# Latent attention by keys: scores with keys on partitions, the maximum as a product row, no turned probabilities

## The chip, the cores and the metric

The kernel runs on one core of a Trainium2 chip. A core has a matrix engine (PE, with a separate weight load PEld), a vector engine (DVE), a scalar engine (ACT), a general engine (POOL) and DMA engines whose queues are issued from SP, ACT and POOL. The metric is the device time of one execution in microseconds; three executions of the kernel before gave 1923.1 to 1924.48 us with a median of 1923.17 us.

## The reference, cut to what matters

The model has two blocks. The change touches one part of the second block, the latent attention: 8 heads, 512 queries of the sequence, 768 keys (512 of the sequence and 256 of a context), head size 96 (64 from a latent, 32 rotary), value size 64. Cut from the reference:

```python
qa_n, qa_r = mla_q(cq, g_cq[i], w_uq[i])
ka_n, va = mla_kv(ckv, g_ckv[i], w_ukv[i])
ka = jnp.concatenate([ka_n, jnp.broadcast_to(ka_r, ka_n.shape[:-1] + (MLA_ROPE,))], axis=-1)
...
# block_attention, for every head, with mla_scale = 96 ** -0.5:
#   softmax over the 768 keys of (q k^T * mla_scale), then times v
```

The result of every head is multiplied with a gate (silu of a projection called za) and goes on into the output projection. Next to it stands a neighbourhood attention over the same sequence, with its own queries, keys and gates, which runs after the latent attention in the kernel.

## The kernel before, in words

Products that must be exact to about single precision are split: every operand is a high and a low part, and one product is three matrix multiplies (`mm3`, L130 to L132), high by high, high by low and low by high. Smaller products whose operands aren't split go through `mm` (L127) in plain single precision; each of these is two records in the trace. A transpose is a multiply with a unit matrix called `ident`, a part of a tile that the trace names `cst`.

`latent()` works on 4 pairs of heads. For each pair `keys(pr)` computes the keys of both heads (96 rows of which 32 are copied by POOL), as a high and a low tile `kT`. For each pair and each tile of 128 queries `queries(pr, t)` transposes the queries and splits them into `qT`. Then, for each of the 32 combinations of pair, query tile and head:

- `scores(n)` multiplies 128 queries (on partitions) with 768 keys, three multiplies of 512 and three of 256 columns, into a tile of two banks (`sc`). DVE reduces it to the negative maximum (L1699), and ACT takes the exponential with that maximum as bias and adds up the sums (L1701).
- `turn(n)` turns the probabilities P so that keys come onto partitions: six transposes (L1709), copied out of the banks by ACT (L1711, four tiles) and DVE (L1713, two tiles) as PT.
- `pv(n)`, once for both heads of a pair, multiplies PT with the values `va`, 12 products of 128 columns, the two heads on the two halves of the partitions. When a pair is done the reciprocals of its sums (DVE, L1728) are spread by small products to all rows (`spread`, L272, L273 and L127 with `rT`) and multiplied in.

Beside it there is work that has no part in the latent attention, the fills: projections of the block's input, written behind `latent()` in the code in the order `A G10 Q K G00 V` (gate za, one further gate, queries, keys, another gate, values of the neighbourhood attention). They use a bank of their own (`fl`). The order of instructions on each engine is not that of the code: a scheduler with a time model places them, so that a fill can stand between steps of the latent attention. Gate blocks are 24 multiplies of 512 columns that end in a tanh on ACT (L1650); the tile `zaT` receives gate za.

Tiles live in pools with a fixed number of buffers for each tag (`b8`: 3, `kt`: 5, `P`: 2 and so on). A tile that finds no free buffer makes its first writer wait for the last reader of an older one.

Of the kernel before, what the change touches and what calls it, by code (L numbers as in the profile page):

```python
# [34 lines left out]
PB2=6  # L35
PXE=1
# [5 lines left out]
MPS=dict(sc=2,po=1,fl=1)  # L42
MKT=5
MP=2
MPT=4
MQT=4
MQ1=5
# [31 lines left out]
def body(ctx, tc, a, stop=None, dump=None):  # L79
# [1432 lines left out]
    xd = dram.tile([128, 4, 1024], F32, name="xd")  # L1512
    nc.scalar.dma_start(xd, x)
# [13 lines left out]
    pm = pools3["u2"] = Pool("pm", "right", {"kr": 3, "kt": MKT, "P": MP, "PT": MPT, "b12": 1, "u2": 2, "qt": MQT, "q1": MQ1})  # L1527
# [103 lines left out]
    def tok_fill(x0, dst, scale=1.0):  # L1631
        for i in range(2):
            w = w3.pair(x0 + 2 * i)
            for t0, nt, p in tok_block(w, 256, hT, tag="fl"):
# [8 lines left out]
    def gate_fill(x0, z):  # L1643

        for m in range(4):
            p = ps(tag="fl")
# [20 lines left out]
    def latent():  # L1667
        kT, qT, PP, PT, sums = {}, {}, {}, {}, {}
        subs = [(pr, t, i) for pr in range(4) for t in range(4) for i in range(2)]

        def keys(pr):
            ks = [[pm("kt", [96, 768], F32R, "kT") for _ in range(2)] for _ in range(2)]
# [5 lines left out]
            for i in range(2):  # L1678
                kT[2 * pr + i] = ks[i]
                for j in range(2):  # L1680
                    G.tensor_copy(ks[i][j][64:96], krT[64 - 32 * j:96 - 32 * j])

        def queries(pr, t):
            p = ps((128, 4, 128), tag="tn")
            for i in range(2):
                T.transpose(p[:96, i], qtok[pr][:, t, i], ident)
            q = qT[pr, t] = [pm("qt", [96, 2, 128], F32R, "qT") for _ in range(2)]
            evac_hl(q[0], q[1], p[:96, :2])

        def scores(n):  # L1690
            pr, t, i = subs[n]
            k, q = kT[2 * pr + i], qT[pr, t]
            p = ps((128, 1024), tag="sc")[:, :768]
            if t + i == 0:
                sums[pr] = sm.tile([128, 8], F32, name=nm("sx"), tag="sx8")
            m = sm.tile([128, 1], F32, name=nm("mx"), tag="mx1")
# [418 lines left out]
```

## Time and profile before

| | before |
|---|---|
| median of three executions | 1923.17 us (1923.1 to 1924.48) |
| the profiled execution | 1923.06 us, of which the span of the trace is 1921.3 us |
| PE busy | 1743.1 us, 91% of the span |
| DVE, ACT, POOL busy | 672.0, 496.5 and 238.6 us |
| from the first query transpose to the end of the latent attention | 1453.60 to 1656.40 us |
| multiplies in this stretch (records) | 1541 |

The span runs from the first to the last instruction of the trace; what lies outside it is 1.76 us. A row of the trace's timeline gives a start and a duration; multiplies are pipelined, so the price of one is the distance between the starts of two, not its duration. In a row with a bracket, the number in it is the time that the engine had stood idle, and the name behind the arrow is what ended that.

### The profile page before, as it was taken

The page shows a single profiled execution, that of the slowest core. Times are in us where ns is not written, and L with a number is a line of the kernel's source. Part 1 is how long each engine was busy: PE and PEld are TensorE (multiplying, and loading weights), DVE is VectorE, ACT ScalarE, POOL GpSimd, SP SyncE. Part 2 cuts the span into 40 slices and gives each one's busy share as a digit, 9 for nine tenths or more (in the row PEclk, how much of TensorE's full clock was granted, in tenths as well). Part 3 has the DMA queues.
Part 4 walks back from the last instruction along what each step waited for, and adds up shares of the span by engine and source line. Part 5 has one row for each costly group of instructions (what it writes and reads, how often), then busy time and mean ns, then how long its engine had stood idle before and what let it go on. Part 6 is the DMA issues. An engine that isn't in the chain of part 4 may idle for free.

```text
span 1921.3 us, 24683 instructions
## 1 busy us (share of the span) xinstructions
PE 1743.1 (91%) x10244; PEld 1081.6 (56%) x10244; DVE 672.0 (35%) x1392; ACT 496.5 (26%) x973; POOL 238.6 (12%) x265
## 2 busy tenths in 40 slices
PE   6998999989999897988888889787899999999998
PEld 5984579963433232322323223222387888888878
DVE  5696686550110101111010110100444333544665
ACT  4335534521000000000000000000545444344433
POOL 2371101000000000000000000000003111333351
PEclk9998999989999999999999999999999999999999
DMA  6322613468999999999999999999622202332232
GB/s 214 105 88 94 192 56 100 175 264 369 425 426 427 426 425 428 424 427 427 425 425 427 427 425 426 427 426 425 242 72 55 56 23 58 89 96 85 79 112 86
DMA packets 95760, 498.39 MB, mean 259 GB/s; under 512 B 6565, under 2 KB 56577, under 8 KB 67233
## 3 DMA queue, kind: packets, MB, share of 16 engines
q1 hardware_dynamic: 90656, 479.06, 62.7%
q0 software_dynamic: 3408, 11.93, 1.9%
q10 hardware_dynamic: 1584, 5.83, 0.8%
q8 instruction: 80, 1.31, 0.3%
q14 instruction: 32, 0.25, 0.0%
HBM read 490.08 MB, written 5.67 MB: 258 GB/s over the span
## 4 chain that ended last, share of the span: by engine, by line
PE 50%; DMA 40%; DVE 5%; ACT 2%; issue 1%; POOL 1%; SPq 0%; DVEq 0%; ACTq 0%; POOLq 0%
DMA we<-in_expert_w_dram 37%; PE ps L127 21%; PE ps L130 8%; PE ps L131 8%; PE ps L132 8%; PE ps L1709 1%; DMA w<-in_ca_wkv_dram 1%; DMA w<-in_w_out_dram 1%; DVE wl L230 1%; PE ps L1867 1%; PE ps L748 1%; ACT wh L229 1%; DMA voff<-vb 1%; DVE qkc L526 1%; POOL sq L458 0%
## 5 line engine op out<-in xcount | busy, mean ns | idle before, releaser
L127 PE MATMUL ps<-we,xe 128*64 128x512 f32 x2048 | 460.7, 597 | 62.7 <-DMA we<-in_expert_w_dram 62.6
L127 PEld LDWEIGHTS ps<-we,xe 128*64 128x64 f32 x2048 | 142.6, 137 | 355.3 <-issue 263.6
L127 PE MATMUL ps<-we,hT 128*64 128x512 f32 x1024 | 233.4, 598 | 29.4 <-DMA we<-in_expert_w_dram 22.8
L127 PEld LDWEIGHTS ps<-we,hT 128*64 128x64 f32 x1024 | 69.8, 136 | 162.8 <-issue 129.7
L229 ACT ACTIVATE wh<-w 128x1024 fp32r<-128x1024 f32 (+4 forms) x100 | 103.9, 1041 | 119.4 <-PE ps L131 74.9
L1303 DVE TENSOR_TENSOR hid<-hid,ps 128x512 f32<-128x512 f32 x32 | 22.0, 687 | 322.1 <-PE ps L127 300.6
L1345 DVE SCALAR_TENSOR_TENSOR y<-ps,gate,y 64x512 fp32r<-64x512 f32 x32 | 24.0, 749 | 313.0 <-ACT y L1344 313.0
L1311 ACT ACTIVATE hT<-ps 128x512 f32<-128x512 f32 x32 | 19.1, 597 | 423.2 <-PE ps L1309 423.2
L301 POOL DMA_DIRECT2D gg<-in_rows_dram x2 | 1.1, 547 | 903.2 <-DMA we<-in_expert_w_dram 903.2
L230 POOL TENSOR_TENSOR wl<-w,wh 128x1024 fp32r<-128x1024 f32 (+1 forms) x34 | 82.7, 2433 | 232.1 <-ACT wh L229 209.5
L230 DVE TENSOR_TENSOR wl<-w,wh 128x1024 fp32r<-128x1024 f32 (+4 forms) x62 | 82.6, 1334 | 69.9 <-ACT wh L229 67.3
L1344 ACT ACTIVATE y<-ps,gate 64x512 fp32r<-64x512 f32 x32 | 21.8, 682 | 260.7 <-PE ps L127 247.6
L130 PE MATMUL ps<-hTh,wh 128*128 128x512 f32 x192 | 76.7, 399 | 1.7 <-ACT va L1624 1.7
L131 PE MATMUL ps<-hTl,wh 128*128 128x512 f32 x192 | 76.0, 396 | 0.0
L132 PE MATMUL ps<-hTh,wl 128*128 128x512 f32 x192 | 75.9, 396 | 0.0
L127 PEld LDWEIGHTS ps<-otT,xn 128*128 128x128 f32 x512 | 60.4, 194 | 24.3 <-issue 22.2
L130 PE MATMUL ps<-wh,hTh 128*128 128x256 f32 (+1 forms) x224 | 68.0, 303 | 0.1
L131 PE MATMUL ps<-wl,hTh 128*128 128x256 f32 (+1 forms) x224 | 67.1, 300 | 0.0
L127 PE MATMUL ps<-otT,xn 128*128 128x128 f32 x512 | 66.0, 284 | 1.0 <-ACT otT L1250 1.0
L132 PE MATMUL ps<-wh,hTl 128*128 128x256 f32 (+1 forms) x224 | 65.6, 298 | 0.0
L1262 DVE TENSOR_TENSOR xe<-ps,cols 128x512 f32<-128x512 f32 (+1 forms) x18 | 10.2, 598 | 144.3 <-PE ps L127 144.3
L1302 ACT ACTIVATE hid<-ps 128x512 f32<-128x512 f32 x32 | 19.1, 596 | 158.4 <-PE ps L127 158.4
(570 smaller groups left out, 3367.4 us busy)
## 6 DMA issues: line engine op xcount, KB each, us to landing
we<-in_expert_w_dram SPq DMA_DIRECT2D x171, 2048.0 KB, 34.4
we<-in_expert_w_dram SPq DMA_DIRECT2D x42, 1024.0 KB, 34.4
w<-in_w_in_dram SPq DMA_DIRECT2D x48, 512.0 KB, 3.8
w<-in_w_mod_dram SPq DMA_DIRECT2D x24, 512.0 KB, 4.3
w<-in_w_out_dram SPq DMA_DIRECT2D x16, 512.0 KB, 3.6
w<-in_ca_wkv_dram SPq DMA_DIRECT2D x8, 512.0 KB, 5.0
wcv<-in_ctx_kv_dram SPq DMA_DIRECT2D x2, 2048.0 KB, 21.4
bm<-in_bias_dram POOLq DMA_DIRECT2D x16, 256.0 KB, 3.2
```

The source lines that it names most:

```text
L127: T.matmul(out, l, r, start=st, stop=sp)
L130: T.matmul(out, L[0], R[0], start=st, stop=False)
L131: T.matmul(out, L[0], R[1], start=False, stop=False)
L132: T.matmul(out, L[1], R[0], start=False, stop=sp)
L229: S.activation(h, w, AF.Copy)
L230: (G if (self.ns % 3 == 2 if self is ws else W3E(self.ns)) else V).tensor_sub(l, w, h.bitcast(F32))
L526: V.scalar_tensor_tensor(o, u[:, 6 + j:518 + j], conv(m, j), o, op0=OP.mult, op1=OP.add)
L748: T.transpose(pp[:, j], st[u][hf][:, tsl(j)], ident)
L1303: V.tensor_mul(h, h, pu)
L1344: S.activation(Y[q][r, 2 * d], p[r], AF.Copy, scale=g)
L1345: V.scalar_tensor_tensor(Y[q][r, 2 * d + 1], p[r], g, Y[q][r, 2 * d].bitcast(F32), op0=OP.mult, op1=OP.subtract)
L1709: T.transpose(p[:, j], P[:, tsl(c0 + j)], ident)
```

## The change

- Scores are computed with keys on partitions: a unit is a pair of heads and one half (256) of the queries, and for each of 6 tiles of 128 keys there are six multiplies of 256 columns, three for each head, both heads side by side in one bank. The exponential goes from there straight to P, without bias and without a sum, and P is multiplied with the values as it stands. The turned probabilities (`turn`, PT) are gone.
- The maximum that was the bias comes first, in products of its own: `peak` multiplies the high parts alone, queries on partitions, 512 and 256 columns, into a bank pair (`mx`) that exists once; DVE reduces it (L1710), and `peak_rows` turns the negative maxima into two rows (two small products with `ident`, an ACT copy, L1716) that stand as rows 96 and 97 under the queries. The keys have in the same rows a 1 for their head and a 0 for the other, so that the product adds the maximum.
- The sums: DVE adds the P tiles of a unit (five additions, L1744); `close` adds over partitions with a product of ones (L127), takes the reciprocal of all 128 x 256 (L1752) and multiplies it in (L1756). `spread` isn't used here any more.
- Buffers: the queries of a whole pair lie in one tile, pairs 0 and 2 in the pool `p3` (`b4`), pairs 1 and 3 in `p3m` (`b8`, 3 buffers), where `zaT` also lies. The `b4` buffers held the context's keys and values of the neighbourhood attention, which are now written to memory (two ACT DMAs) and read back behind the latent attention (two POOL DMAs). `sc` is now two single banks, `mx` takes two. Fill blocks take their bank by a cycle `fl` (five times), then `fl, sc, sc`.

```diff
@@ constants
+NFL=5
-MPS=dict(sc=2,po=1,fl=1)
-MKT=5
-MP=2
-MPT=4
-MQT=4
-MQ1=5
+MPS=dict(sc=2,mx=1,po=1,fl=1)
+MKT=8
+MP=8
+MQ1=3
...
+    fills = itertools.chain(["fl"] * NFL, itertools.cycle(("fl", "sc", "sc")))
+        if tag == "fx":
+            tag = next(fills)
...
+    nc.scalar.dma_start(cbd[:, 0], ckb)
+    nc.scalar.dma_start(cbd[:, 1], cvb)
...
+                G.tensor_copy(ks[i][0][96:98], ident[96:98, 96 + i:97 + i].to_broadcast([2, 768]))
 
         def queries(pr, t):
+            if t == 0:
+                if pr % 2:
+                    b = p3m("b8", [98, 2, 2, 512], F32R, "qT")
+                    qT[pr] = b[:, 0], b[:, 1]
+                else:
+                    qT[pr] = [p3("b4", [98, 2, 512], F32R, "qT") for _ in range(2)]
+                mx[pr] = sm.tile([128, 4, 2], F32, name=nm("mx"), tag="sx8")
...
-        def scores(n):
...
-            for c in (slice(0, 512), slice(512, 768)):
-                mm3(p[:, c], [v[:, i] for v in q], [v[:, c] for v in k], True, True)
-            V.tensor_reduce(m, p, axis=AX.X, op=OP.max, negate=True)
-            P = PP[n] = pm("P", [128, 768], F32, "P")
-            S.activation(P, p, AF.Exp, bias=m, accum_out=sums[pr][:, 2 * t + i:2 * t + i + 1])
-
-        def turn(n):
...
-                for j in range(c):
-                    T.transpose(p[:, j], P[:, tsl(c0 + j)], ident)
...
+        def peak(pr, t, i):
+            p = ps((128, 1024), tag="mx")[:, :768]
             for c in (slice(0, 512), slice(512, 768)):
+                mm(p[:, c], qT[pr][0][:96, i, tsl(t)], kT[2 * pr + i][0][:96, c], True, True)
+            V.tensor_reduce(mx[pr][:, t, i:i + 1], p, axis=AX.X, op=OP.max, negate=True)
+
+        def peak_rows(pr, f):
+            p = ps((128, 4, 128), tag="tn")
+            for t in range(2):
+                mm(p[96:98, t], mx[pr][:, 2 * f + t], ident, True, True)
+            S.activation(qT[pr][0][96:98, :, 256 * f:256 * f + 256],
+                         p[96:98, None, 0:2].rearrange("p a t c -> p a (t c)").to_broadcast([2, 2, 256]), AF.Copy)
...
+        def scores(pr, f, j):
+            p = ps((128, 2, 256), tag="sc")
+            c = slice(256 * f, 256 * f + 256)
+            for i in range(2):
+                (kh, kl), (qh, ql) = kT[2 * pr + i], qT[pr]
+                mm(p[:, i], kh[:98, tsl(j)], qh[:98, i, c], True, False)
+                mm(p[:, i], kh[:96, tsl(j)], ql[:96, i, c], False, False)
+                mm(p[:, i], kl[:96, tsl(j)], qh[:96, i, c], False, True)
+            o = P[j] = pm("P", [128, 2, 256], F32, "P")
+            S.activation(o, p, AF.Exp)
+
+        def pv(pr, f, j):
...
+            for i in range(2):
+                mm(po[pr][64 * i:64 * i + 64, 256 * f:256 * f + 256],
+                   va[:, j, 128 * pr + 64 * i:128 * pr + 64 * i + 64], o[:, i], j == 0, j == 5)
+            if j == 0:
+                acc[0] = o
+            else:
+                V.tensor_add(acc[0], acc[0], o)
+
+        def close(pr, f):
+            p = ps(tag="sc")
+            for i in range(2):
+                mm(p[64 * i:64 * i + 64, :256], ones[:, :64], acc[0][:, i], True, True)
+            r = pm("P", [128, 512], F32, "rs")
+            V.reciprocal(r[:, :256], p[:, :256])
...
+            V.scalar_tensor_tensor(oaT[-1][:, c], po[pr][:, c], 0.5, r[:, :256], op0=OP.mult, op1=OP.mult)
...
+        for n, u in enumerate(units):
+            g = first(*units[n + 1]) if n < 7 else iter(())
             for j in range(6):
+                scores(*u, j)
+                next(g, 0)
+                if j:
+                    pv(*u, j - 1)
+            pv(*u, 5)
+            for _ in g:
+                pass
+            close(*u)
...
+    ckb, cvb = (p3("b4", [128, 2, 512], F32, n) for n in ("ckb", "cvb"))
+    nc.gpsimd.dma_start(ckb, cbd[:, 0])
+    nc.gpsimd.dma_start(cvb, cbd[:, 1])
     nc.gpsimd.dma_start(voff[0:64, 1:5], vb[64:128])
     nc.gpsimd.dma_start(voff[64:128, 0:4], vb[0:64])
```

`first(pr, f)` is a generator that yields after the keys and after each of four peaks: `keys` (for the first half), the two query tiles with two peaks each, then `peak_rows`. The loop takes a step of the next unit's `first` between the key tiles of this one.

How this stands in the engines' rows is shown at three places. The first is PE at the start of the latent attention, in the kernel before: `ps_8486` and `ps_8498` are scores of the first two heads, `ps_9656` is the second block of the fill for gate za.

```order
L1686 MATMUL ps_8479<-cst,qtok_8250 96x128 [waits DVE_49,PE_49]
L1686 MATMUL ps_8479<-cst,qtok_8250 96x128
L130 MATMUL ps_8486<-kT_8448,qT_8475 128x512 [waits Activation_49,Pool_49]
L131 MATMUL ps_8486<-kT_8449,qT_8475 128x512 [waits Pool_49]
L130 MATMUL ps_8498<-kT_8450,qT_8475 128x512 [waits Pool_49]
L132 MATMUL ps_8486<-kT_8448,qT_8476 128x512 [waits DVE_49]
L130 MATMUL ps_8486<-kT_8448,qT_8475 128x256
L131 MATMUL ps_8486<-kT_8449,qT_8475 128x256
L132 MATMUL ps_8486<-kT_8448,qT_8476 128x256
L130 MATMUL ps_9656<-hTh_7777,wh_8427 128x512 [waits DVE_49]
L131 MATMUL ps_9656<-hTl_7778,wh_8427 128x512
```

And now: `ps_8485`, `ps_8489`, `ps_8498` and `ps_8502` are the peaks of the first unit, `ps_8506` its maximum rows, `ps_8519` and `ps_8553` query tiles of the second unit, `ps_8524` a peak of the second unit, `ps_8510` the first scores.

```order
L131 MATMUL ps_8498<-kT_8451,qT_8477 128x512 [waits DVE_49,Activation_49]
L131 MATMUL ps_8498<-kT_8451,qT_8477 128x256
L131 MATMUL ps_8506<-cst,mx_8479 2x128
L1702 MATMUL ps_8519<-cst,qtok_8253 96x128 x2
L131 MATMUL ps_8502<-kT_8453,qT_8477 128x512 [waits DVE_49]
L131 MATMUL ps_8502<-kT_8453,qT_8477 128x256
L1702 MATMUL ps_8553<-cst,qtok_8253 96x128 [waits DVE_49]
L1702 MATMUL ps_8553<-cst,qtok_8253 96x128
L131 MATMUL ps_8506<-cst,mx_8479 2x128 [waits DVE_49]
L131 MATMUL ps_8524<-kT_8451,qT_8477 128x512 [waits PE_49,Activation_49]
L131 MATMUL ps_8524<-kT_8451,qT_8477 128x256
L131 MATMUL ps_8510<-qT_8477,kT_8451 128x256 [waits Activation_49]
```

The first scores moved behind four peaks, each of which waits for DVE's reduction of the one before, and behind the rows; between them stands no fill. The next fill block, `ps_9457`, now stands some 370 rows further on, in the first half of pair 2, and in between PE's rows hold the latent attention alone.

The second place is ACT, at the tanh of the first fill block (`zT`, gate za), in the kernel before, at the start of the latent attention:

```order
L135 ACTIVATE kT_8450<-ps_8460 64x256 [waits DVE_49]
L135 ACTIVATE qT_8475<-ps_8472 96x256 [waits PE_49]
L1650 ACTIVATE zT_9628<-ps_9629 128x512 [waits DMASW5_49,PE_49,Activation_49]
L135 ACTIVATE qT_8482<-ps_8479 96x256 [waits PE_49]
L1701 ACT_TABLE_LOAD
L1701 ACTIVATE P_8496,sx_8487<-ps_8486,mx_8488 128x768 [waits DVE_49]
L229 ACTIVATE wh_9690<-w_8437 128x1024 [waits DMAHW5_49,PE_49,Activation_49]
L1701 ACTIVATE P_8507,sx_8487<-ps_8498,mx_8499 128x768 [waits DVE_49]
L1711 ACTIVATE PT_8520<-ps_8521 128x512 [waits PE_49]
L1650 ACTIVATE zT_9628<-ps_9656 128x512 [waits PE_49]
```

And now, at the start of pair 3's queries (`qT_9152`), while the exponentials of pair 2 run:

```order
L139 ACTIVATE kT_9119<-ps_9129 64x256 [waits DVE_49]
L1732 ACTIVATE P_9115<-ps_9108 128x512 [waits PE_49]
L139 ACTIVATE qT_9152<-ps_9154 96x2x128 [waits PE_49]
L1657 ACTIVATE zT_9429<-ps_9430 128x512
L1732 ACTIVATE P_9150<-ps_9143 128x512 [waits PE_49,Activation_49]
L1732 ACTIVATE P_9172<-ps_9165 128x512 [waits PE_49,Activation_49]
L139 ACTIVATE qT_9152<-ps_9190 96x2x128 [waits PE_49]
L1732 ACTIVATE P_9188<-ps_9181 128x512 [waits PE_49,Activation_49]
```

The tanh that frees the bank `fl` stood behind the first query copy of the latent attention and now stands behind the first query copy of pair 3, since `zT` takes the buffer of pair 1's queries.

The third place is DVE between the second half of pair 1 and the first half of pair 2. `P_8870` holds the sum of the P tiles, `mx_8909` the maxima of pair 2, `rs_8996` the reciprocals of the unit that ends.

```order
L1744 TENSOR_TENSOR P_8870<-P_8870,P_8965 128x512 [waits DVE_49,Activation_49]
L1744 TENSOR_TENSOR P_8870<-P_8870,P_8981 128x512 [waits DVE_49,Activation_49]
L1710 TENSOR_REDUCE mx_8909<-ps_8951 128x1 [waits PE_49]
L140 TENSOR_TENSOR qT_8908<-ps_9008,qT_8907 96x2x128 [waits Activation_49]
L1752 RECIPROCAL rs_8996<-ps_8993 128x256 [waits PE_49]
L1710 TENSOR_REDUCE mx_8909<-ps_8967 128x1 [waits PE_49]
L140 TENSOR_TENSOR qT_8908<-ps_9042,qT_8907 96x2x128 [waits Activation_49]
L1756 SCALAR_TENSOR_TENSOR oaT_8861<-ps_8785,rs_8996 128x256 [waits DVE_49]
```

In the kernel before DVE had these rows at the end of pair 0; `mx_8637` and `mx_8659` are maxima of the next pair's and this one's scores, `sx_8487` the sums of pair 0.

```order
L1699 TENSOR_REDUCE mx_8637<-ps_8636 128x1 [waits DVE_49,PE_49]
L1713 COPY PT_8647<-ps_8654 128x256 [waits PE_49]
L1699 TENSOR_REDUCE mx_8659<-ps_8658 128x1 [waits DVE_49,PE_49]
L1713 COPY PT_8669<-ps_8676 128x256 [waits PE_49]
L1728 RECIPROCAL sx_8487<-sx_8487 128x8 [waits Activation_49]
```

Before, reductions alternate with copies and the reciprocal is one of 128 x 8; now the reduction of the next unit's last peak (`ps_8967`) stands behind a reciprocal of 128 x 256.

## Rows read from the trace of the kernel before

**Rows 1.** The page: span, and the chain that ended last.

```profile
span 1921.3 us, 24683 instructions
...
PE 50%; DMA 40%; DVE 5%; ACT 2%; issue 1%; POOL 1%; SPq 0%; DVEq 0%; ACTq 0%; POOLq 0%
```

**Rows 2.** The latent attention's stretch by engine: busy (records), clock, DMA, GB/s.

```profile
1453.60:1656.40 202.80, 202.60 (x1541) 173.01 (x1539) 70.69 (x115) 92.82 (x172) 35.47 (x26) 1.00 0.16 45
```

**Rows 3.** Groups of the stretch: busy, mean ns, idle ahead and its releaser.

```profile
L127 PE MATMUL ps<-PT,va 128*64 128x128 f32 x384 | 34.2, 282 | 0.0
L1709 PE MATMUL ps<-cst,P 128*128 128x128 f32 x192 | 31.4, 276 | 0.0
L1699 DVE TENSOR_REDUCE mx<-ps 128x1 f32<-128x768 f32 x32 | 30.5, 953 | 44.7 <-PE ps L132 44.6
...
L1701 ACT ACTIVATE P<-ps,mx 128x768 f32<-128x768 f32 x32 | 28.9, 902 | 44.0 <-DVE mx L1699 29.7 <-PE ps L1709 14.2
...
L1711 ACT ACTIVATE PT<-ps 128x512 f32<-128x512 f32 x32 | 19.0, 595 | 25.1 <-PE ps L1709 24.7
```

**Rows 4.** PE's timeline, steady and around one value product: start, duration.

```profile
1512.45 0.28 PE L130 MATMUL ps<-wh,hTh 128*128 128x256 f32 x1
1512.66 1.09 PE L127 MATMUL ps<-PT,va 128*64 128x128 f32 x16
1513.69 0.27 PE L272 MATMUL ps<-cst,sx 128*8 128x128 f32 x1
...
1514.71 0.39 PE L130 MATMUL ps<-wh,hTh 128*128 128x256 f32 x1
1514.93 0.28 PE L131 MATMUL ps<-wl,hTh 128*128 128x256 f32 x1
```

**Rows 5.** PE's timeline: spread, 256-wide splits, transposes.

```profile
1515.97 1.09 PE L127 MATMUL ps<-rT,cst 8*64 8x128 f32 x16
1516.99 0.42 PE L1686 MATMUL ps<-cst,qtok 128*96 128x128 f32 x2
...
1518.20 0.28 PE L132 MATMUL ps<-wh,hTl 128*128 128x256 f32 x1
...
1519.99 0.28 PE L132 MATMUL ps<-wh,hTl 128*128 128x256 f32 x1
...
1524.69 0.60 PE L1709 MATMUL ps<-cst,P 128*128 128x128 f32 x4
1525.22 0.43 PE L127 MATMUL ps<-PT,va 128*64 128x128 f32 x2
```

**Rows 6.** The chain, in order of time, behind the stretch: start, length.

```profile
1658.22 11.53 DMA voff<-vb
...
1673.09 0.23 PE ps L130
```

**Rows 7.** Timelines of DVE and PE at that point.

```profile
1669.88 0.06 DVE L1810 MEMSET obT<- 128x1 f32 x1 [2.52 <-DMA voff<-vb]
...
1671.25 0.66 PE L1799 MATMUL ps<-cst,tk 128*128 128x128 f32 x4 [1.82 <-DVE kn L1801]
```

**Rows 8.** Groups of the whole run: reciprocals, an addition in SBUF, an exponential.

```profile
L136 DVE TENSOR_TENSOR ymTl<-sg,ymTh 128x512 fp32r<-128x512 f32 x4 | 2.6, 678 | 0.0
...
L736 DVE RECIPROCAL rx<-sx 128x2 f32<-128x2 f32 x16 | 2.5, 159 | 3.5 <-ACT P L733 3.5
...
L1728 DVE RECIPROCAL sx<-sx 128x8 f32<-128x8 f32 x4 | 0.8, 203 | 2.8 <-ACT P L1701 2.8
...
L1858 ACT ACTIVATE P<-ps,mx 128x512 f32<-128x512 f32 x32 | 21.8, 685 | 25.3 <-DVE mx L1856 25.1
```

**Rows 9.** Windows in which PE thinned out: busy, then clock.

```profile
1388.50:1391.90 3.40, 1.00 (x4) 0.21 (x3) 2.58 (x8) 3.10 (x12) 0.00 (x0) 1.00 0.00 0
1391.90:1395.30 3.40, 1.80 (x8) 1.40 (x8) 1.38 (x6) 1.86 (x7) 0.00 (x0) 0.50 0.00 0
1395.30:1398.70 3.40, 2.23 (x10) 2.24 (x11) 1.55 (x5) 1.68 (x6) 0.00 (x0) 0.50 0.00 0
```

More of the change, by code (lines that the diff above doesn't have):

```diff
@@ L1667, in latent @@
     def latent():
-        kT, qT, PP, PT, sums = {}, {}, {}, {}, {}
-        subs = [(pr, t, i) for pr in range(4) for t in range(4) for i in range(2)]
+        kT, qT, mx = {}, {}, {}
         def keys(pr):
-            ks = [[pm("kt", [96, 768], F32R, "kT") for _ in range(2)] for _ in range(2)]
+            ks = [[pm("kt", [98, 768], F32R, "kT") for _ in range(2)] for _ in range(2)]
             for s in (slice(0, 512), slice(512, 768)):
@@ L1717, in pv @@
-        def pv(n):
-            pr, t, _ = subs[n]
-            if t == 0:
-                po[pr] = ps((128, 4, 128), tag="po")
-            pts = PT.pop(n - 1), PT.pop(n)
-            for j in range(6):
-                for i in range(2):
-                    mm(po[pr][64 * i:64 * i + 64, t], va[:, j, 128 * pr + 64 * i:128 * pr + 64 * i + 64],
-                       pts[i][:, j], j == 0, j == 5)
-            if t == 3:
-                r = sums.pop(pr)
-                V.reciprocal(r, r)
-                o = p3m("b3", [128, 512], F32, "oaT")
-                oaT.append(o)
-                o = o.rearrange("p (t c) -> p t c", t=4)
-                S.activation(o, po.pop(pr), AF.Copy)
-                V.tensor_mul(o, o, spread(r, "tn", pm("q1", [8, 128], F32, "rT"), 0.5))
@@ L1735, in latent @@
-        keys(0)
-        queries(0, 0)
-        queries(0, 1)
-        scores(0)
-        scores(1)
-        for n, (pr, t, i) in enumerate(subs):
-            if n + 2 < len(subs):
-                scores(n + 2)
-            turn(n)
-            if i:
-                pv(n)
-                u = 4 * pr + t + 2
-                if u < 16:
-                    queries(*divmod(u, 4))
-            if t == 2 and i and pr < 3:
-                keys(pr + 1)
+            q = qT[pr]
+            evac_hl(q[0][:96, :, tsl(t)], q[1][:96, :, tsl(t)], p[:96, :2])
@@ new lines, in first @@
+        def first(pr, f):
+            if f == 0:
+                keys(pr)
+                yield
+            for t in (2 * f, 2 * f + 1):
+                queries(pr, t)
+                for i in range(2):
+                    peak(pr, t, i)
+                    yield
+            peak_rows(pr, f)
+        units = [(pr, f) for pr in range(4) for f in range(2)]
+        for _ in first(0, 0):
+            pass
+        for n, u in enumerate(units):
+            g = first(*units[n + 1]) if n < 7 else iter(())
+            for j in range(6):
+                scores(*u, j)
[4 more added lines that the diff above has]
+            for _ in g:
+                pass
+            close(*u)
@@ L1763, in body @@
         elif v == "A":
-            gate_fill(X["A"], lambda m: zaT[:, m])
+            gate_fill(X["A"], lambda m: zaT[:, m], "fx")
         else:
-            gates((int(v[1]), int(v[2])), lambda: next(room), "fl")
+            gates((int(v[1]), int(v[2])), lambda: next(room), "fx")
     for m in range(4):
```

38 lines of the change are left out of this document (15 added, 23 removed).

## The prediction

> **What bounds the kernel now.** I read the page first: the chain that ended last is PE for half of the span and DMA for most of the rest [rows 1]; the DMA part is the experts' weights in the middle, which this change doesn't touch. Then I read the stretch of the latent attention by engine: PE is busy 202.60 of 202.80 us at full clock, while DVE has 70.69, ACT 92.82 and POOL 35.47 us of work [rows 2]. So this stretch is bound by PE, through the fills that stand between the attention's own steps. A saved multiply is worth its distance on PE's timeline, nothing that DVE or ACT lose is worth anything, and a wait counts as soon as PE has nothing to put into it. Last I read the groups of the stretch: DVE waits 44.6 us for scores and ACT 29.7 us for the maxima [rows 3]; those are idle times of engines that don't bound.
>
> **Prices.** Steady split products of 256 columns: fifteen steps from 1518.20 to 1519.99, .119 us each [rows 5]; of 512 columns: .23 [rows 6]. Four transposes from 1524.69 to 1525.22: .53, of which about .09 is the entry (below), so .11 each [rows 5]. Sixteen records of a value product take 1.03 us (1512.66 to 1513.69), or about .11 for a pair of heads and .15 for the group. The step from a split product into it is .21 where .12 is usual (+.09), and the split product behind it takes .22 (+.10) [rows 4]. Four spreads, one of them 1.02 us [rows 5].
>
> **PE's sum.** Removed: 192 transposes by .11, -21.1; four spreads, -4.1. Scores: 32 x 3 x (.23 + .119) = 33.3 before, 48 tiles x 6 x .119 = 34.3 now, +1.0. Value products: the same columns, 0. Added: 32 peaks x (.23 + .119) = +11.1; rows, 16 products of two records by .107, +3.4; `close`, 8 units by .43 (two records for a pair of 256 columns, twice the .21 that a pair of 256 would take by the .11 above), +3.4. Together -6.3. Changes between split and plain groups: by the order, 47 of the 56 plain groups follow a split product now and 50 are followed by one, against 21 and 18 of 48. 26 x .09 + 32 x .10 + 8 x .15 = 6.7 more, from which the edges of the removed transposes go. Some 34 entries of transposes by .09 are saved (-3.1) and a few exits (-.4): I take +3.2 and keep 0 and 6.7 as ends. PE's work then falls by 3.1 us.
>
> **Waits.** The order shows the three places. First, the start. Four peaks go through one bank pair, so each waits for the reduction of the one before: .35 for the products, some .2 until DVE sees them, .95 for the reduction [rows 3], .07 back, 1.6 us a turn. With the last rows' product and its way to ACT (.45) and an ACT copy of 512 columns (.6 [rows 3]) 7.45 us pass. In these PE has 3.35 us of work: five peaks 1.75, query transposes and rows 1.1, the end of the first fill block .5. It has no more, since the second fill block can't start: its bank is held until a tanh that stands on ACT behind pair 3's first query copy. +4.1. The ends are 2 (if the reductions overlap with more of PE's query work) and 5.
>
> Second, the end of a unit: the last peak's reduction waits on DVE behind a reciprocal of 128 x 256, and behind it stand the rows, ACT's copy and the next unit's scores. Reciprocals take 159 ns for 2 columns and 203 for 8 [rows 8], 7.3 ns a column, so 256 columns take about 2.0 us by that slope; a reduction of 768 columns at 953 ns is 1.24 ns a column [rows 3], which for 256 columns would give .35 and is the lower end. I take 1.9, just under the slope of the same operation. The Trainium skill ("VectorE: DVE Perf Modes", section "First, the fixed hardware budget") says that the reciprocal is an iterative divide with a repeat count of 8. By that rule an estimate of eight passes at the reduction's 1.24 ns a column would be 2.5 us, .6 more at that one place. The trace agrees in so far as the slope is several times that of a reduction. At the end of unit (1,1), the second half of pair 1, the order puts it so: 1.9 + .95 + .07 + .2 + .6 = 3.7 us to the next scores, less .9 of transposes, rows and one peak, +2.8. At the end of (0,1) the reduction is ahead: 1.8 less .5, +1.3. In the three first halves without fills the keys' products lie between, and I put +.5 each. In all 5.6 (ends 2 and 9). Fills come back only in the first half of pair 2, and from there waits cost nothing.
>
> DVE does in a unit 4 reductions by .95, 5 additions by .68 (the nearest row is a subtraction in SBUF [rows 8]), the reciprocal, and low parts of queries and keys and the last product, some 1500 columns by 1.24 ns: 3.8 + 3.4 + 1.9 + 1.9 = 11.0 us. PE does 12.3: six tiles by .71 and .43, four peaks 1.4, `close`, rows and transposes 1.6, keys half the time (1.1), edges 1.4. ACT has six exponentials of .69 at most [rows 8], 4.1 us, and some copies. Neither binds by these sums. The turned copies that go (32 on ACT at .6 [rows 3]) free engines that waited.
>
> Third, a wait that goes. Behind the stretch the chain waits 11.53 us for `voff<-vb` [rows 6]; a DVE memset stands behind that transfer and holds DVE 2.52 us, PE 1.82 us and a little more after it [rows 7]. In the new order the fills run alone behind the last unit, gate and query projections first, and the memset has 12 to 13 us of PE work in front of it where the transfer needs 11.5; -2.2. The two new transfers into memory stand in the stretch of the cross attention, where nothing reads them; the two back are issued by POOL at about .55 each ahead of `voff`'s, +0 as long as that cover of 1 us or so holds, and +1.1 otherwise. The fills that then run alone cost PE what they cost before: moving them is 0, with the weight splits ahead of them.
>
> **The sum.** -6.3 + 3.2 + 4.1 + 5.6 - 2.2 = +4.4. On the profiled execution's own time, 1923.06 us (a span of 1921.3 [rows 1] and 1.76 around it, .1 below the median), that is 1927.5.
>
> **Rivals.** *Faster.* The groups change for nothing, the units' waits overlap, and only the start costs: -6.3 + 4.1 - 2.2 = -4.4, 1918.7. For it: the stretch of before holds its 202.60 us of PE work with .2 of idle although it has such edges all along [rows 2]. Against it: the .21 and .22 are paid there too, inside the busy time [rows 4], and the units without fills have little that could overlap.
>
> *Slower: DVE becomes the bound of the units without fills.* If an addition takes 1.1 us in place of .68, which decides from about .94 us on (11.0 + 5 x .26 = 12.3), a unit takes 13.1 on DVE plus the hand-offs that can't overlap, 2 to 3 us over PE's 12.3 in five and a half units, +11 to +16 in place of the 5.6: 1933 to 1938, about 1936. For it: the unit is a ring (peak, reduction, rows, scores, exponential, addition) with one `mx` buffer. Against it: POOL, whose work slows DVE's in SBUF, has only key copies there.
>
> *The clock.* In the cross attention's end PE was busy 1.00 of 3.40 us at full clock, and the granted clock then read 0.50 for the two windows behind it although PE did more [rows 9]; of the two levels that is 1.2 GHz. The start has 3.35 us of PE work in 7.45 us. If the clock falls there for some 7 us, 7 us of PE's work behind it take up to twice as long, less what lies in waits: +3.5 to +5, 1932. The Trainium skill ("TensorE: Matmul & The Clock Gate", section "Loop structure matters more than you think") says that matmuls stay warm only if the loop nest leaves no long waits between them, and that PE goes cold otherwise. No row here has a start like this one, so the trace neither bears that out for it nor excludes it.
>
> *The waits don't vanish at `voff`*, because POOL issues two more transfers first: +1.1 to +2.2, 1929.2; this lies in the first case's range.
>
> **How the numbers follow.** Forecast with its own range, 1922 to 1932: .47. Faster, 1914 to 1920: .24. DVE bound, 1932 to 1940: .17. Clock, 1929 to 1936: .12. The range from 1917 to 1937 takes about 8 in 10. A measurement of this kernel can tell 0.2%, 3.85 us. Below 1919.3: .25, nearly all of it the faster case. Above 1927.0: half of the first case (.24) and the two slow ones but for their edge, .45. Between: .30.
>
> **What the profile after would show.** PE's idle time at the start of the latent attention should be about 4 us, released by DVE's reduction and ACT's copy of rows; the reciprocal's row should read 1.8 to 2.1 us; DVE's additions about .68; no bracket of 1.8 us at the key transposes behind the stretch; the transposes L1709 and 21 us of them gone, and 11 us of peaks in their place. I am wrong if PE's idle in the units without fills is under 2 or over 12 us, if the clock in the first 20 us reads .5, or if plain groups are entered without loss.

## The result, and the profile after

The changed kernel takes 1942.67 us (median of four executions, 1938.70 to 1946.94) against 1923.74 us before: a ratio of 1.0099, 95% interval 1.0076 to 1.0122. It is slower by about 19 us, outside the forecast's range of 1917 to 1937. The profiled execution is the shortest of the four; these are the page's span, its first section's PE and its chain:

```profile
span 1936.9 us, 24224 instructions
...
PE 1751.3 (90%) x10016; PEld 1066.7 (55%) x10016; DVE 699.8 (36%) x1404; ACT 480.3 (25%) x929; POOL 246.6 (13%) x275
...
PE 48%; DMA 39%; DVE 6%; ACT 3%; POOL 2%; issue 2%; SPq 0%; DVEq 0%; ACTq 0%; POOLq 0%
```

PE has 228 records fewer and is busy 8 us longer. To see where, one stretch is cut out of each kernel between two marks that both have: from the first fill product (the one that had waited for `va`) to the last turned tile of the neighbourhood attention. The windows of before, then of after (columns as in [rows 2]):

```profile
1449.18:1824.40 375.22, 372.67 (x2616) 311.29 (x2617) 164.94 (x283) 166.29 (x318) 102.38 (x87) 1.00 0.24 68
```

```profile
1445.93:1840.60 394.67, 381.71 (x2388) 299.35 (x2389) 192.37 (x295) 149.75 (x274) 108.16 (x96) 0.97 0.23 67
```

The stretch grew by 19.5 us, all of the loss. (The profiled execution reached it 3.2 us earlier than that of before, so the spans differ by 15.6 only; the kernels below that change the attention alone reach it anywhere from 1445.7 to 1458.5 us.) Idle time is the length less PE's busy time: 2.5 us before, 13.0 after. What the clock cost is put down as the sum, over windows of one microsecond, of PE's busy time times one less the granted clock: 0 before, 13.2 after. What is left counts as PE's work at full clock:

| | length | PE's work | idle | clock |
|---|---|---|---|---|
| before | 375.2 | 372.7 | 2.5 | 0.0 |
| after | 394.7 | 368.5 | 13.0 | 13.2 |
| difference | +19.5 | -4.2 | +10.5 | +13.2 |

The three parts add up by their definition, and this account takes a microsecond at 0.50 for half a microsecond of work. By the rows it is a little more: the four records of a value product take 1.05 us from start to start at the low level and .58 at the full one, and over 17 kinds of rows that four of the profiles have at both levels the ratio is 1.78 (89.6 us against 50.4). So the clock's column, here and in the table further down, is an eighth too high, and the work's is too low by as much. As an estimate, the clock cost some 11.6 us after, and PE's work is 370.1, or 2.6 us below before's. The kernel below whose clock never fell agrees: its work is 378.3 us, of which some 7.5 are products that nobody reads, so 370.8.

So the attention's products did become cheaper, by some 2.6 us; waits ate that four times over, and the clock as much again and more. PE's longer waits are these on its timeline:

```profile
1453.64 0.59 PE L131 MATMUL ps<-kT,qT 96*128 96x512 f32 x2 [1.14 <-POOL kT L1689]
...
1455.37 0.59 PE L131 MATMUL ps<-kT,qT 96*128 96x512 f32 x2 [1.14 <-DVE mx L1710]
...
1459.06 0.59 PE L131 MATMUL ps<-cst,mx 128*2 128x128 f32 x2 [0.62 <-DVE mx L1710]
...
1520.27 0.38 PE L131 MATMUL ps<-cst,mx 128*2 128x128 f32 x2 [1.90 <-DVE mx L1710]
...
1558.76 0.38 PE L131 MATMUL ps<-cst,mx 128*2 128x128 f32 x2 [2.87 <-DVE mx L1710]
```

What goes through `mm` stands at L131 now (plain products, but also the scores and peaks, whose operands are split parts), what goes through `mm3` at L134 to L136. The first three waits are two of the first unit's peaks and its maximum rows, behind the key copies of POOL or the reduction of a peak; the last two are the maximum rows at the ends of two units, (1,1) and (2,1). In windows of 3.4 us the clock falls at each of the three places, to the level of 1.2 GHz; at the start it does so behind the second row:

```profile
1456.80:1460.20 3.40, 2.57 (x8) 1.48 (x8) 1.85 (x4) 1.13 (x3) 0.00 (x0) 0.50 0.00 0
1460.20:1463.60 3.40, 3.40 (x16) 3.06 (x14) 0.96 (x1) 2.26 (x4) 0.00 (x0) 0.50 0.00 0
...
1470.40:1473.80 3.40, 3.40 (x11) 1.90 (x12) 1.68 (x3) 0.59 (x1) 0.00 (x0) 0.51 0.00 0
1473.80:1477.20 3.40, 3.40 (x25) 2.04 (x24) 2.25 (x3) 1.79 (x3) 0.00 (x0) 1.00 0.00 0
1518.00:1521.40 3.40, 1.36 (x9) 0.57 (x6) 3.03 (x5) 0.97 (x2) 2.31 (x3) 1.00 0.02 5
1521.40:1524.80 3.40, 3.40 (x16) 2.96 (x18) 0.79 (x1) 1.20 (x2) 0.00 (x0) 0.51 0.00 0
1524.80:1528.20 3.40, 3.40 (x14) 1.85 (x14) 1.73 (x3) 0.60 (x1) 0.00 (x0) 0.50 0.00 0
...
1555.40:1558.80 3.40, 0.53 (x5) 0.28 (x4) 3.40 (x4) 0.44 (x2) 0.00 (x0) 1.00 0.68 195
1558.80:1562.20 3.40, 3.40 (x10) 2.60 (x11) 2.12 (x4) 0.59 (x1) 1.28 (x1) 0.53 0.16 56
```

Five windows at the low level after the start, two after (1,1), one after (2,1). In a window at 0.50 PE looks fully busy, 3.40 of 3.40, and does little more than half of the work (16 records where the first window back at 1.00 has 25). Busy time alone hides this loss.

Two groups of DVE in this stretch, to be held against the forecast's prices:

```profile
L1744 DVE TENSOR_TENSOR P<-P,P 128x512 f32<-128x512 f32 x40 | 28.8, 720 | 24.7 <-ACT P L1732 17.6 <-PE ps L131 5.8 <-ACT zT L1657 1.1
L1752 DVE RECIPROCAL rs<-ps 128x256 f32<-128x256 f32 x8 | 14.0, 1756 | 4.4 <-PE ps L131 4.3
```

### The profile page after: what moved, and what is told of

Same layout as the page of the kernel before. It is cut to its first block, busy times and chain, and to the rows that moved or that the text cites. A ratio compares the mean times of both kernels' runs of the same rounds, so it can differ in the third digit from the quotient of the medians.

```text
span 1936.9 us, 24224 instructions
## 1 busy us (share of the span) xinstructions
PE 1751.3 (90%) x10016; PEld 1066.7 (55%) x10016; DVE 699.8 (36%) x1404; ACT 480.3 (25%) x929; POOL 246.6 (13%) x275
## 4 chain that ended last, share of the span: by engine, by line
PE 48%; DMA 39%; DVE 6%; ACT 3%; POOL 2%; issue 2%; SPq 0%; DVEq 0%; ACTq 0%; POOLq 0%
DMA we<-in_expert_w_dram 37%; PE ps L131 24%; PE ps L134 7%; PE ps L135 7%; PE ps L136 7%; DMA w<-in_ca_wkv_dram 1%; DMA w<-in_w_out_dram 1%; DVE wl L234 1%; PE ps L1902 1%; ACT wh L233 1%; PE ps L752 1%; POOL wl L234 1%; DVE qkc L530 1%; DMA voff<-vb 1%; POOL sq L462 0%
## 5 line engine op out<-in xcount | busy, mean ns | idle before, releaser
L131 PE MATMUL ps<-we,xe 128*64 128x512 f32 x2048 | 464.8, 602 | 59.6 <-DMA we<-in_expert_w_dram 59.6
L131 PEld LDWEIGHTS ps<-we,xe 128*64 128x64 f32 x2048 | 144.3, 138 | 354.7 <-issue 263.7
L131 PE MATMUL ps<-we,hT 128*64 128x512 f32 x1024 | 233.2, 598 | 28.2 <-DMA we<-in_expert_w_dram 21.6
L131 PEld LDWEIGHTS ps<-we,hT 128*64 128x64 f32 x1024 | 69.8, 136 | 161.5 <-issue 128.3
L134 PE MATMUL ps<-hTh,wh 128*128 128x512 f32 x192 | 76.5, 399 | 1.7 <-ACT va L1631 1.7
L136 PE MATMUL ps<-hTh,wl 128*128 128x512 f32 x192 | 75.8, 397 | 0.0
L131 PEld LDWEIGHTS ps<-otT,xn 128*128 128x128 f32 x512 | 60.7, 195 | 24.0 <-issue 21.9
L131 PE MATMUL ps<-otT,xn 128*128 128x128 f32 x512 | 66.3, 285 | 1.0 <-ACT otT L1254 1.0
L134 PE MATMUL ps<-wh,hTh 128*128 128x256 f32 (+1 forms) x224 | 66.2, 297 | 0.0
L136 PE MATMUL ps<-wh,hTl 128*128 128x256 f32 (+1 forms) x224 | 64.9, 295 | 0.0
```

Source lines behind the costliest of these rows:

```text
L131: T.matmul(out, l, r, start=st, stop=sp)
L134: T.matmul(out, L[0], R[0], start=st, stop=False)
L136: T.matmul(out, L[1], R[0], start=False, stop=sp)
```

## The experiments

Two theories stood against each other. *Clock*: thin places, where no fill stands, let PE's clock fall, and the work behind them runs at half speed. *Waits*: the idle time and what hangs on it are the whole loss. Below, "before" is the kernel before, timed on the same chip beside each group of runs: 1923.5 to 1925.1 us.

**Fills from the start.** Gate za's tile is what blocks the fills' bank, so its fill goes behind others:

```diff
-MORD='A G10 Q K G00 V'
+MORD='G10 Q K A G00 V'
-NFL=5
+NFL=16
```

> The changed kernel, but the fill for gate za stands behind the other gate, the queries and the keys, and the first 16 fill blocks use the bank of the fills alone, so that fills stand between the attention's steps from its start. Theory clock (PE thins out where no fill stands, its granted clock falls to 0.50 and the work behind runs at half speed): no window of the latent attention below 0.95, PE idle there under 2 us, and since the profile of the changed kernel has some 13 us of loss by the clock and 10 us of idle, about 1920 us (1915 to 1924). Theory waits (the low clock costs little, the 10 us of idle and what hangs on them are the loss): about 1933 us, with or without a low clock. Theory products (PE's own work is dearer than before): 1938 us or more.

Measured: 1928.17 us (1922.29 to 1937.88), ratio to before 1.0028 (1.0010 to 1.0046). Of the stretch 4.6 us are idle, the clock costs 3.4, and PE's work is 372.3, not 368.5. 14 us of the loss are gone with the same attention. It isn't the 1920 of the clock theory: the first peaks still thin PE out (1.6 us of idle, and behind them all of the clock's loss), and edges between plain and split products come back with the fills: on its timeline PE goes from split to plain products 113 times in this stretch, 103 times after and 116 times before. Two lines were changed at once, the order and the number of blocks in the fills' own bank; which of them gave what is not shown.

**Useless work at the start.** Thirteen products that nobody reads, after the first three peaks:

```diff
+        NW = [5, 5, 3, 0]
+
+        def warm(t, n):
+            p = ps(tag="po")
+            for _ in range(n):
+                mm(p, qT[0][0][:96, 0, tsl(t)], kT[0][0][:96, :512], True, True)
...
                     peak(pr, t, i)
+                    if pr + f == 0 and t + i < 2:
+                        warm(t, NW[2 * t + i])
```

> The changed kernel with 13 more products of 512 columns, whose result nobody reads, in the gaps between the first peaks of the latent attention; they cost about 3 us if they don't fit into the gaps. Theory clock: the granted clock stays at 1.00 through the first unit, the 17 us at half speed there go, and with them 7 to 8 us: about 1935 us. Theory waits: the gaps are only filled, the time stays at 1942 to 1946 us.

Measured: 1937.76 us (1932.90 to 1946.34), 5 us less than the changed kernel with 3 us more of work; against before the ratio is 1.0071 (1.0046 to 1.0096) where the changed kernel has 1.0099 (1.0076 to 1.0122), so the gain isn't clear of noise. Windows of the start, and of the place behind the end of (1,1):

```profile
1453.40:1460.20 6.80, 6.05 (x30) 3.66 (x28) 4.90 (x7) 1.04 (x3) 3.63 (x5) 1.00 0.29 77
1460.20:1467.00 6.80, 6.66 (x43) 4.68 (x43) 3.87 (x5) 4.16 (x6) 0.00 (x0) 1.00 0.00 0
1518.20:1531.80 13.60, 13.60 (x49) 8.07 (x49) 5.39 (x8) 3.74 (x7) 0.00 (x0) 0.50 0.00 1
```

The fall at the start is gone. The one behind (1,1) lasted far longer in this execution than in the changed kernel's, so only part of the gain stayed: the loss by the clock is 11.9 us, and the waits at the ends of (1,1) and (2,1) are those of the changed kernel, 1.90 and 2.87 us.

**Closing a unit later**, behind the next unit's first scores:

```diff
                 scores(*u, j)
+                if j == 0 and n:
+                    close(*units[n - 1])
                 next(g, 0)
...
-            close(*u)
+        close(*u)
```

> The changed kernel, with each unit closed (sum product, reciprocal, last product) behind the first scores of the next unit, so that no reduction of a last peak stands behind the reciprocal. Theory clock: the idle of 1.9 us and 2.9 us before the rows of pairs 2 and 3 goes, and with it the two falls of the clock behind them (10 us at half speed): 8 to 10 us, about 1933 us. Theory waits: 4 to 5 us, about 1938 us.

Measured: 1946.81 us (1943.34 to 1947.43). Both theories missed. The two long waits are gone, but others came in their place, as on its timeline:

```profile
1493.01 0.42 PE L1702 MATMUL ps<-cst,qtok 128*96 128x128 f32 x2 [0.96 <-DVE qT L140]
1493.88 0.38 PE L131 MATMUL ps<-cst,mx 128*2 128x128 f32 x2 [0.44 <-DVE mx L1710]
```

Idle is 12.7 us against the changed kernel's 13.0, and the clock fell in more places (17.9 us). The reciprocal's place in DVE's order isn't the cause of the idle time: with the reciprocal moved, units without fills waited for DVE elsewhere.

**No peaks.** No products, reductions or rows for the maximum; the two rows are zero and the exponential is taken of a 64th of the score.

```diff
         def peak(pr, t, i):
-            p = ps((128, 1024), tag="mx")[:, :768]
-            for c in (slice(0, 512), slice(512, 768)):
-                mm(p[:, c], qT[pr][0][:96, i, tsl(t)], kT[2 * pr + i][0][:96, c], True, True)
-            V.tensor_reduce(mx[pr][:, t, i:i + 1], p, axis=AX.X, op=OP.max, negate=True)
+            pass
...
+            V.memset(qT[pr][0][96:98, :, 256 * f:256 * f + 256].bitcast(F32), 0.0)
...
-            S.activation(o, p, AF.Exp)
+            S.activation(o, p, AF.Exp, scale=2.0 ** -6)
```

> The changed kernel without peaks: no products, reductions and rows for the maximum; the two rows are zero, and the exponential is taken of a 64th of the score. PE loses 14.5 us of products. Theory clock: idle of 8 to 10 us and the low clock go too, 13 us or more: about 1906 us (1902 to 1911). Theory waits: 14.5 and 10 us, about 1918 us. If neither holds and only the products count: 1928 us.

Measured: 1908.19 us (1904.63 to 1912.75). PE's work falls to 350.0 us, 18.5 less than after. Idle is 12.0 us, and the clock's loss falls to 3.3. Three of the waits are these:

```profile
1458.79 0.40 PE L1702 MATMUL ps<-cst,qtok 128*96 128x128 f32 x2 [1.75 <-DVE kT L140]
...
1481.29 0.65 PE L131 MATMUL ps<-P,cst 128*64 128x256 f32 x4 [1.66 <-DVE P L1737]
...
1659.98 1.33 PE L1827 MATMUL ps<-cst,tk 128*128 128x128 f32 x5 [3.12 <-DVE kc L1829]
```

The last lies behind the attention, at the key transposes of [rows 7], and has 1.6 of the clock's loss behind it. Up to 1598 us it is 8.9 us of idle and 1.7 of clock, against 11.2 and 13.2 of the changed kernel. The total is that of the clock theory, but not by its terms: most of the waits didn't go. So nearly equal idle time goes with far less clock loss; it matters how it lies. Here it is spread over more pieces, and the clock fell briefly behind two of them (1.66 and 3.12 us) and not behind another of 1.75.

**Fills spread further.** Of orders of the fills, one that by the rows leaves no long gap:

```diff
-MORD='A G10 Q K G00 V'
+MORD='Q G10 K G00 A V'
-NFL=5
+NFL=16
```

> The changed kernel with the fills in another order (queries, one gate, keys, the other gate, then gate za, values) and the first 16 blocks in the fills' own bank: by the order 56 fill products stand among the first peaks, 535 in the whole latent attention, and no stretch of more than 34 rows is without one. Theory clock, with what the last four runs showed (PE's work 364 us where it stands alone, 368 with fills between): clock at 1.00 throughout, idle under 3 us, work 368 us: about 1921 us (1918 to 1924), and little spread between runs. If the peaks' ring costs time even beside fills: 1926 us or more.

Measured: 1922.72 us (1920.20 to 1929.38), ratio 0.9989 (0.9972 to 1.0006): 20 us less than the changed kernel, no difference from before that can be told. The stretch:

```profile
1450.78:1829.40 378.62, 374.71 (x2388) 294.55 (x2389) 195.32 (x295) 149.30 (x274) 109.95 (x96) 1.00 0.24 70
```

Idle 3.9, clock 1.7, work 373.0: what PE saved is gone where fills stand between (120 changes from split to plain products, 103 in the changed kernel). Of the idle time 1.7 us, and with it all of the clock's loss, lie behind the attention, at the key transposes. (The expectation's 364 and 368 us of work are counted from the first query transpose, some 4.5 us later than the stretch here.)

**The old attention without fills.** The kernel before, with buffers held so that gate za's tile comes free only at pair 3's first query copy, as in the changed kernel:

```diff
+        held = {u: p3m("b8", [128, 4, 512], F32, "held") for u in ((3, 0), (3, 2), (3, 3))}
+        for v in held.values():
+            G.memset(v[:96, 0, 0:1], 0.0)
...
+            if (pr, t) in held:
+                S.activation(held[pr, t][:96, 0, 0:1], p[:96, 0, 0:1], AF.Copy)
```

> The kernel before, with buffers held so that gate za's tile comes free only at pair 3's first query copy, as in the changed kernel: no fill from the first fill block on until pair 3, and the attention itself as it was. Theory clock: the old attention alone leaves PE idle for DVE's reductions and the turned copies as well, 10 us or more over six pairs' worth of steps, and the clock falls: 1938 us or more. Theory new attention (the loss lies in the peaks' ring, and the fills' absence only shows it): under 1930 us.

Measured: 1953.33 us (1949.79 to 1962.11), ratio 1.0147. The stretch has 24.2 us of idle and 6.7 us of clock loss. Some 12.7 of the idle lie behind 1600 us, where the fills run alone; up to 1598 us, where they come back, it is 11.5 of idle and 5.0 of clock; the changed kernel has 11.2 and 13.2 up to the same time. So the old attention waits as long without fills, and the idle time is no property of the new one; what is its own, in these profiles, is that the waits lie where the clock falls further. (Its work, 377.5 us, is 4.8 above before's with fewer changes between split and plain products, 93; what is dearer there stays open.)

**More useless work**, eight products near the end of each of five units, on top of the thirteen.

```diff
+            if 0 < 2 * pr + f < 6:
+                p = ps(tag="sc")
+                for _ in range(8):
+                    mm(p, qT[pr][0][:96, 1, tsl(2 * f + 1)], kT[2 * pr + 1][0][:96, :512], True, True)
```

> The kernel with 13 unread products at the start, and 40 more, eight near the end of each of five units that have no fill beside them: 9 us of useless work. Theory clock: the useless work fills gaps and keeps the clock up, its loss falls from 12 to 3 us or less, and the time falls by some 3 to 8 us, to about 1932 us. Theory waits: the useless work can only fill gaps or come on top: 1938 to 1947 us.

Measured: 1944.21 us (1941.13 to 1957.00), as the waits theory had it. But the products don't stand in the gaps: they depend on nothing late, so the order puts them ahead of the last peak, and the waits remain:

```profile
1522.54 0.43 PE L131 MATMUL ps<-cst,mx 128*2 128x128 f32 x2 [1.90 <-DVE mx L1710]
...
1565.16 0.38 PE L131 MATMUL ps<-cst,mx 128*2 128x128 f32 x2 [2.87 <-DVE mx L1710]
```

Behind the first of them the clock stood at the low level for some 14 us, behind the second it didn't fall in this profile. The products missed the gaps, so this run doesn't decide.

**Useless work in the gaps.** The thirteen at the start, and repeats of the sum product at the ends of (1,1) and (2,1), where they depend on the last addition:

```diff
+        NX = {3: 4, 5: 6}
...
             close(*u)
+            if n in NX:
+                p = ps(tag="sc")
+                for _ in range(NX[n]):
+                    for i in range(2):
+                        mm(p[64 * i:64 * i + 64, :256], ones[:, :64], acc[0][:, i], True, True)
```

> The changed kernel with unread products in the three gaps in which PE thinned out: 13 of 512 columns among the first peaks, and the sum product of `close` repeated 4 and 6 times at the ends of units (1,1) and (2,1), where PE stood 1.9 and 2.9 us. Theory clock: the low clock goes in all three places (13 us in the profile of the changed kernel), of 6 us of useless work about 5 lie in idle time: about 1930 us (1926 to 1934), and the granted clock reads 1.00 there. Theory waits: the useless work only replaces idle time or comes on top: 1940 to 1946 us.

Measured: 1936.28 us (1929.47 to 1940.20), while the changed kernel itself, run again beside it, took 1944.34 us (1940.78 to 1954.39):

> The changed kernel as it is, for comparison on the same chip: 1938 to 1947 us, and the longer of its executions with the lower mean clock.

The stretch of this kernel, its place after the start, that behind (1,1) and that behind (2,1), in windows:

```profile
1458.50:1842.70 384.20, 378.35 (x2441) 297.22 (x2442) 192.63 (x295) 149.63 (x274) 107.53 (x96) 1.00 0.24 69
```

```profile
1471.20:1478.00 6.80, 6.57 (x43) 4.40 (x43) 3.78 (x7) 4.11 (x6) 0.00 (x0) 1.00 0.00 0
1524.00:1530.80 6.80, 5.83 (x43) 3.61 (x39) 4.78 (x6) 2.17 (x4) 2.48 (x4) 1.00 0.00 0
1566.00:1572.80 6.80, 6.80 (x41) 5.16 (x40) 3.20 (x4) 2.80 (x5) 1.27 (x1) 1.00 0.00 0
```

The stretch is 384.2 us against 397.7 of the changed kernel run beside it: with some 7.5 us of useless products (10 us more of work by the account) it is 13.5 shorter, since idle fell from 13.0 to 5.9 and the clock's loss from 16.7 to nothing. (At (2,1) a fill block moved into the gap too.) In the total, three of six executions lie at 1929 to 1933, and three at 1940, among them the profiled one: it reached the stretch 12.8 us later than the changed kernel's, so its excess arose ahead of it. For the other two that isn't shown.

**Without the memset.** `V.memset(obT[:, 0, 0:1], 0.0)` was the instruction behind which DVE waited for `voff<-vb`; the column is written later anyway. It is taken out of the spread version, and out of the kernel before:

> The kernel with the fills spread (the run before named so) without the memset of one column of obT, behind which DVE waited 4 us for a transfer (the column is written later in any case). The stall of PE behind it, 1.7 us, and what it did to the clock go: 1.7 to 3.5 us less than with it, about 1920 us. If the wait for the transfer only moves to another instruction: no change, 1922 to 1923 us.

> The kernel before without the same memset: its stall of 2.35 us on PE goes, about 1921 us; if the wait only moves: no change.

Measured: 1919.50 us (1918.05 to 1923.91), ratio to before 0.9981 (0.9970 to 0.9992), for the spread version; 1922.50 us (1918.56 to 1933.66), ratio 0.9995 (0.9977 to 1.0013), for the old one. Neither can be told from its kernel with the memset: the spread version had 0.9989 (0.9972 to 1.0006), and the old one's interval holds 1. In the profiles the stall is gone from the spread version, and the clock's loss with it (the stretch is 374.9 us in place of 378.6). It is the fastest kernel here that computes the maximum, 0.2% below before, and of those with twelve executions it has the narrowest range. Its stretch is no shorter than the old one's:

```profile
1446.63:1821.50 374.87, 372.68 (x2388) 293.28 (x2389) 194.71 (x294) 149.22 (x274) 109.73 (x96) 1.00 0.25 71
```

```profile
1448.63:1822.70 374.07, 372.47 (x2617) 311.32 (x2617) 165.94 (x282) 166.30 (x318) 102.91 (x87) 1.00 0.24 68
```

In the profiles it reaches the stretch 2.0 us earlier and takes 1.3 us less behind it, and it lacks the old one's long executions; what makes its median 3 us lower was not settled.

The stretches together (us, from the profiled executions; work and clock by the account above, with its error of an eighth of the clock's column):

| kernel | median | length | work | idle | clock |
|---|---|---|---|---|---|
| before | 1923.74 | 375.2 | 372.7 | 2.5 | 0.0 |
| after | 1942.67 | 394.7 | 368.5 | 13.0 | 13.2 |
| after, again | 1944.34 | 397.7 | 368.0 | 13.0 | 16.7 |
| fills from the start | 1928.17 | 380.3 | 372.3 | 4.6 | 3.4 |
| useless work at the start | 1937.76 | 394.0 | 371.6 | 10.5 | 11.9 |
| closing later | 1946.81 | 398.2 | 367.6 | 12.7 | 17.9 |
| no peaks | 1908.19 | 365.4 | 350.0 | 12.0 | 3.3 |
| fills spread | 1922.72 | 378.6 | 373.0 | 3.9 | 1.7 |
| old attention, fills held | 1953.33 | 408.4 | 377.5 | 24.2 | 6.7 |
| more useless work | 1944.21 | 398.2 | 381.4 | 10.1 | 6.7 |
| useless work in the gaps | 1936.28 | 384.2 | 378.3 | 5.9 | 0.0 |
| spread, no memset | 1919.50 | 374.9 | 372.7 | 2.2 | 0.0 |
| before, no memset | 1922.50 | 374.1 | 372.5 | 1.6 | 0.0 |

## Why the prediction was wrong

- **The clock: the step that failed.** The sum had no term for it; it stood as a rival at a chance of .12, with one fall at the start, "some 7 us" long and worth 3.5 to 5 us. Measured were falls in three places, 17, 7 and 3 us long, 13.2 us in one profile and 16.7 in the next (some 11.6 and 14.6 by the rows' prices). That 11.6 is most of the 15.1 us between the forecast's +4.4 and the stretch's +19.5; the rest is idle time, +10.5 for +7.5, and .5 of PE's work. One of the forecast's own signs of being wrong, a clock of .5 in the first 20 us, came. That the falls come from the gaps is shown by the last useless work: gaps filled, clock at 1.00 in all three places. The Trainium skill ("TensorE: Matmul & The Clock Gate", section "Loop structure matters more than you think") says that long waits between matmuls let PE go cold. The trace agrees in the direction: the window with 1.90 us of idle in it (PE busy 1.36 of 3.40 us) was followed by one at 0.51.
- **PE's work** was put at -3.1 and came out at some -2.6, which is partly luck. The edges between groups, taken at +3.2, had the wrong sign: PE goes from split to plain products 103 times in the stretch after and 116 times before, which by the prices of [rows 4] is 2.5 us less (an estimate). So the products must have cost some 6 us more than priced. Part of that are the peaks with their rows, 18.5 us in the run without them for the 14.5 of the forecast; some 2 of the 18.5 are edges, since that run has 92 such changes. Where the rest lies stays open. The edges depend on the fills: there are 113 and 120 with the fills moved, and work is 372.3 to 373.0 us there, for the 370.1 of the attention alone.
- **Waits** at the start and in the units were put at +9.7 in all, and all idle rose by 10.5. But by place they were off. The start's three rows above have 2.9 us (3.3 with a wait of .38 between them) in place of 4.1, one of them POOL's key copy; the end of (0,1) has none for the 1.3, and the end of (1,1) 1.90 in place of 2.8. "Fills come back only in the first half of pair 2, and from there waits cost nothing" failed twice: the first of these fill products stands at 1542.68 us, 6.4 behind the sum product of (2,0), and at the end of (2,1) PE waited 2.87 us, the longest wait of all, for a reduction that stood on DVE behind a weight split and the reciprocal:

```profile
1555.00 1.23 DVE L234 TENSOR_TENSOR wl<-w,wh 128x1024 fp32r<-128x1024 f32 x1 [0.72 <-ACT wh L233]
1556.15 1.75 DVE L1752 RECIPROCAL rs<-ps 128x256 f32<-128x256 f32 x1
1557.81 0.89 DVE L1710 TENSOR_REDUCE mx<-ps 128x1 f32<-128x768 f32 x1
```

- **The wait that goes** (-2.2, [rows 6, 7]) stayed: PE stood 1.73 us at the same key transposes. The chain, in order of time, shows POOL with a weight split ahead of the transfer's issue; the timelines show the memset behind the transfer, a copy behind the memset, another weight split on POOL beside that copy, and PE's wait:

```profile
1673.72 2.39 POOL wl L234
1676.11 0.21 POOL voff L1818
...
1676.55 10.01 DMA voff<-vb
```

```profile
1680.91 0.43 DVE L1831 COPY tk<-x 128x512 f32<-128x512 f32 x1 [0.54 <-PE ps L1834]
...
1686.68 0.06 DVE L1845 MEMSET obT<- 128x1 f32 x1 [3.94 <-DMA voff<-vb]
1686.77 1.84 DVE L1831 COPY tk<-x 128x512 f32<-128x512 f32 x1
```

```profile
1685.97 2.37 POOL L234 TENSOR_TENSOR wl<-w,wh 128x1024 fp32r<-128x1024 f32 x1 [8.86 <-ACT wh L233]
```

```profile
1689.39 1.27 PE L1834 MATMUL ps<-cst,tk 128*128 128x128 f32 x8 [1.73 <-DVE kc L1836]
```

The cover came out about as forecast: PE had work until 1687.66 us, and the transfer had landed at 1686.56. What the forecast left out is the copy, which took 1.84 us where the same copy took .43 earlier, and ended .27 us behind POOL's split. Had it taken .43, PE would have stood some .3 us (an estimate). With the fills from the start no split ran there: DVE waited 2.44 us for the transfer, the copy took .43, and PE didn't wait behind it.

- **The prices** held: the reciprocal takes 1.756 us for the 1.9 worked out from [rows 8], so the 2.5 that the prediction estimated from the Trainium skill ("VectorE: DVE Perf Modes", section "First, the fixed hardware budget") is too dear here; additions take .72 for .68. DVE as the bound of the units is not borne out, though its latency sets the waits: between the first two falls of the clock, where no fill stands, it is busy 34.86 us and PE 42.63.

```profile
1473.80:1518.00 44.20, 42.63 (x280) 26.91 (x279) 34.86 (x50) 19.35 (x37) 8.94 (x10) 1.00 0.00 1
```

- **The rival that the change is faster** needed the waits to overlap. With fills spread they nearly do, and then the edges take the gain: what is left is no change.

## What to carry to other kernels

Work that has no part in a loop but stands between its steps is cover: when a change moves a tile into another's buffer, see in the order which independent work now waits for it, and price the loop without that work. Price idle time by what the clock does behind it as well, from windows with the granted clock, because busy time looks full at half speed. And when a change saves a few microseconds of multiplies, count its edges in the place where it will stand, beside the fills.

## What the runs showed of the hardware that had not been expected

The time at the low clock differs between executions of one kernel: behind the end of (1,1), with the same 1.90 us of idle, it was 7 us in the changed kernel's first profile and 13.7 in its second, and some 20 us in the kernel with useless work at the start, though PE was busy all through. The changed kernel's ten executions run from 1938.70 us at a mean clock of 0.984 to 1954.39 us at 0.975, nearly all of them longer as the clock is lower.

A copy on DVE from and to SBUF stood as long as a weight split ran on POOL. In nine profiles the copy behind the memset met such a split: it took 1.60 to 2.51 us in place of .43, and ended .27 to .29 us behind the split.
